# PEER expert layers: all activation tiles computed in the routing stage, and an output stage that streams V alone

## The chip, the cores and the metric

The kernel runs on one core of one Trainium2 chip. The metric is device microseconds of one launch. The engines are called here by the profile's names: PE (TensorE; its weight loads are PEld), DVE (VectorE), ACT (ScalarE), POOL (GpSimd) and SP, which only issues DMAs. DMAs are also issued from the queues of ACT and, for gathers by index, of POOL.

## The reference, cut to what matters

The model has two layers over 512 tokens of width 1024: an mLSTM mixer with a PEER expert layer behind it, then stick-breaking attention with a second PEER layer. The change touches the two PEER layers alone. Of 16384 experts (128 x 128 pairs of sub-keys) each token takes 16 in each of 8 heads:

```python
s = jnp.einsum('thpk,pnk->thpn', q, sub_keys)            # 8 heads, 2 sub-key sets, 128 keys
s_top, i_top = lax.top_k(s, 16)
cand = (s_top[:, :, 0, :, None] + s_top[:, :, 1, None, :]).reshape(128, 8, 256)
g_top, pos = lax.top_k(cand, 16)
expert = jnp.take_along_axis(cand_idx, pos, axis=-1)      # cand_idx = i0 * 128 + i1
g = jax.nn.softmax(g_top, axis=-1)
u = jnp.take(peer_u, expert, axis=0)
act = jax.nn.gelu(jnp.einsum('thkd,td->thk', u, xb), approximate=False)
vv = jnp.take(peer_v, expert, axis=0)
return jnp.einsum('thk,thkd->td', g * act, vv)
```

## The kernel before, in words

All of it is float32. A large product is made of three matmuls in a reduced float type: each operand is split into a high part and a remainder (`whi` and `wlo` of a weight, `hh` and `hl` of an activation, `Wh` and `Wl`), and high x high, high x remainder and remainder x high are summed. ACT makes the high part (L98), POOL or DVE the remainder (L99), as the call says.

A PEER layer, `peer(l)`, treats its tokens in two ways. The first 128 tokens (`NGT = 1` tile) are **gathered**: 128 indirect DMAs on POOL fetch one row of U each per token, DVE takes the dot products with the token (L958, into `uw`), and 128 more fetch rows of V, which DVE adds up with weights (L969, into `yt`). Each fetch is 128 rows of 4 KB into one of four `rows` buffers. The other 384 tokens are computed **densely**: the experts come in 128 tiles `a` of 128. For each tile, 24 matmuls of 384 columns give the scores of its experts (L787, into `pp`) and ACT applies GELU (L790, into `ga` or `sp`): here this is called an act. The routing weights of the dense tokens are spread out to a table `Gd` in DRAM. For each token the one-hot of its second key (`oB`) is multiplied with the one-hot of the first key, scaled by the high and the low half of the weight (`oH`, `oL`): two matmuls of 128 columns (L921, L922, into `gps`); ACT copies four tokens at a time to `stg` (L924), and 32 tokens go to `Gd` in one DMA. At last, per tile, `W = ga * gb` with `gb` read back from `Gd` (L995), and 18 matmuls of 512 columns add W times V to the output (L1016, into `y`), two halves of the width for three token tiles.

The layer runs in three parts:

- The query part: 16 projections (L115), scores (L829), and the top 16 of each by `max`, `max_index` and `match_replace` on DVE (`top16`, L656 to L660).
- The **routing stage**, in which PE and DVE keep the order of the program text. `route` (L662 to L755) is a generator: the program advances it by estimated microseconds. First comes the route of token tile 1. Then 48 steps (16 for each token tile 1 to 3, 8 tokens each): the four one-hot tiles on DVE (`oB`, `oA`, `oH`, `oL`, L910 to L913), 2 us of the next tile's `route`, `run(22)`, which emits 22 of the act matmuls, and the 16 matmuls of these 8 tokens. The next tile's route is that of tile 2, of tile 3, and last that of the gathered tile 0. 56 of the 128 acts (`KPRE`) are made in this stage; the first 10 (layer 0) or 18 (layer 1) stay in SBUF, the others go to DRAM (`spd`).
- The **output stage**, ordered by a scheduler: 128 times 18 matmuls of `y`, with the other 72 acts between them, three tiles ahead, and all 256 gathers spread over it. U is loaded for those 72 acts, V for all tiles, both by `wload` (`wraw`, three buffers, split into `whi` and `wlo`, three buffers).

In the first layer a few steps of the next layers' conditioning (`ada`) run along in the background.

## Time and profile before

| what | value |
|---|---|
| three runs | 3381.13, 3384.81, 3403.76 us; median 3384.81 |
| the profiled execution, first to last instruction | 3385.6 us |
| routing stage of layer 0: first act to first `y` matmul | 484.9 to 862.8 us |
| output stage of layer 0: first to last `y` matmul | 862.8 to 1708.6 us |
| the same of layer 1 | 2172.1 to 2539.3, and 2539.3 to 3375.2 us |
| PE busy over the span | 94% |

The profiled span lies 0.8 us from the median, so a sum in the profile's times can be set against the median directly. "Busy" of PE counts modelled matmul ends, and consecutive matmuls overlap; the distance between starts says how fast they follow each other. The granted clock is 1.00 where TensorE had 2.4 GHz throughout, and lower where part of the stretch was granted 1.2 GHz.

### The profile page before, as it was taken

Reading aid. Unit: us, or ns where it says so; the run is one execution under the profiler, and the core shown is the slowest. Engines: PE = TensorE matmul, PEld = TensorE weight load, DVE = VectorE, ACT = ScalarE, POOL = GpSimd, SP = SyncE. Lnnn points to the kernel's source line nnn. Section 1 sums busy time; section 2 is a strip of 40 time slices with the busy share of each in tenths; the row PEclk is TensorE's granted clock in tenths of the full one; section 3 lists DMA queues with packets and bytes.
Section 4 is the critical chain, followed back from the end, with each engine's and each line's share of the span. In section 5 each row is a group of like instructions: output and inputs, shape, how many; then the busy total and the mean of one; then the engine's idle time right before and its main releaser. Section 6 shows DMA issues by size and latency. Waiting matters only on the chain. (4 is left out here: it accounts for less than half of the span.)

```text
span 3385.6 us, 44234 instructions
## 1 busy us (share of the span) xinstructions
PE 3168.3 (94%) x16160; PEld 2704.2 (80%) x16160; DVE 2655.0 (78%) x4484; ACT 1360.5 (40%) x1898; POOL 1729.5 (51%) x1097
## 2 busy tenths in 40 slices
PE   6899998888999999999989999988889999999999
PEld 5746787888888888888867657978888888888888
DVE  6833699998678888888874484899967888888887
ACT  4254324555333333333342453345543333333333
POOL 3434433343456566566553454433344665666664
PEclk9989998999999999999989899989999999999999
DMA  5621453555889999999955102235568999999997
GB/s 194 212 87 44 158 181 125 184 207 194 293 306 328 330 320 326 340 332 317 324 171 192 44 12 78 94 125 192 203 211 292 315 319 320 327 335 336 328 346 262
DMA packets 308363, 787.62 MB, mean 233 GB/s; under 512 B 25136, under 2 KB 145200, under 8 KB 305072
## 3 DMA queue, kind: packets, MB, share of 16 engines
q1 hardware_dynamic: 218864, 449.48, 39.6%
q0 software_dynamic: 73728, 268.47, 22.0%
q10 hardware_dynamic: 15552, 66.85, 5.1%
q8 instruction: 126, 2.06, 0.3%
q14 instruction: 93, 0.76, 0.1%
HBM read 715.76 MB, written 68.94 MB: 232 GB/s over the span
## 5 line engine op out<-in xcount | busy, mean ns | idle before, releaser
L99 POOL TENSOR_TENSOR wlo<-wraw,whi 128x1024 fp32r<-128x1024 f32 x353 | 894.5, 2535 | 1077.4 <-ACT whi L98 1018.5
L98 ACT CAST whi<-wraw 128x1024 fp32r<-128x1024 f32 x609 | 639.3, 1051 | 899.8 <-PE pp L787 230.6
L787 PE MATMUL pp<-hh,wlo 128*128 128x384 f32 x2048 | 704.7, 344 | 9.8 <-POOL wlo L99 9.6
L787 PE MATMUL pp<-hh,whi 128*128 128x384 f32 x2048 | 703.5, 343 | 10.9 <-ACT whi L98 5.2
L787 PE MATMUL pp<-hl,whi 128*128 128x384 f32 x2048 | 701.9, 343 | 0.0
L1016 PE MATMUL y<-wlo,Wh 128*128 128x512 f32 x1536 | 481.5, 392 | 3.4 <-DVE wlo L99 3.2
L1016 PE MATMUL y<-whi,Wl 128*128 128x512 f32 x1536 | 469.2, 392 | 5.8 <-DVE Wl L99 5.8
L958 DVE SCALAR_TENSOR_TENSOR rows<-rows,htok 128x1024 f32<-128x1024 f32 x256 | 380.4, 1497 | 116.5 <-DMA rows<-in_u_rows,pidx 116.1
L1016 PE MATMUL y<-whi,Wh 128*128 128x512 f32 x1536 | 456.8, 393 | 10.2 <-ACT Wh L98 6.4
L951 POOL DMA_INDIRECT rows<-in_v,pidx x256 | 342.1, 1336 | 212.2 <-DVE yt L969 170.2
L951 POOL DMA_INDIRECT rows<-in_u_rows,pidx x256 | 338.9, 1324 | 153.8 <-DVE rows L958 109.6
L787 PEld LDWEIGHTS pp<-hh,wlo 128*128 128x128 f32 x2048 | 395.5, 193 | 22.9 <-POOL wlo L99 18.1
L787 PEld LDWEIGHTS pp<-hh,whi 128*128 128x128 f32 x2048 | 395.4, 193 | 22.7 <-ACT whi L98 6.1
L969 DVE SCALAR_TENSOR_TENSOR yt<-rows,uw,yt 128x1024 f32<-128x1024 f32 x254 | 367.9, 1448 | 49.9 <-DMA rows<-in_v,pidx 47.8
L787 PEld LDWEIGHTS pp<-hl,whi 128*128 128x128 f32 x2048 | 395.5, 193 | 4.6
L99 DVE TENSOR_TENSOR wlo<-wraw,whi 128x1024 fp32r<-128x1024 f32 x256 | 328.7, 1284 | 63.1 <-ACT whi L98 62.5
L1016 PEld LDWEIGHTS y<-whi,Wh 128*128 128x128 f32 x1536 | 287.0, 189 | 67.9 <-ACT Wh L98 10.3
L1016 PEld LDWEIGHTS y<-whi,Wl 128*128 128x128 f32 x1536 | 288.4, 188 | 65.6 <-DVE Wl L99 8.1
L1016 PEld LDWEIGHTS y<-wlo,Wh 128*128 128x128 f32 x1536 | 288.4, 188 | 62.7 <-DVE wlo L99 5.1
L98 ACT CAST Wh<-W 128x384 fp32r<-128x384 f32 x256 | 130.8, 514 | 477.8 <-DVE W L995 462.6
L115 PE MATMUL pp<-hh,whi 128*128 128x512 f32 x584 | 236.9, 413 | 28.0 <-ACT cbuf L349 9.2
L924 ACT ACTIVATE stg<-gps 128x512 f32<-128x512 f32 x192 | 197.5, 1139 | 140.2 <-PE gps L922 137.9
(282 smaller groups left out, 4508.3 us busy)
## 6 DMA issues: line engine op xcount, KB each, us to landing
wraw<-in_u SPq DMA_DIRECT2D x256, 512.0 KB
wraw<-in_v SPq DMA_DIRECT2D x256, 512.0 KB
g<-stg ACTq DMA_DIRECT2D x24, 2048.0 KB
gb<-g SPq DMA_DIRECT2D x64, 768.0 KB
araw<-in_ada_w SPq DMA_DIRECT2D x80, 512.0 KB
wraw<-in_peer_q SPq DMA_DIRECT2D x32, 512.0 KB
spd<-ga ACTq DMA_DIRECT2D x84, 192.0 KB
ga<-spd SPq DMA_DIRECT2D x84, 192.0 KB
```

The lines of the kernel that those rows point to most:

```text
L98: S.copy(hi, src)
L99: eng.tensor_tensor(lo, src, hi.bitcast(F32), op=OP.subtract)
L115: PE.matmul(ps, a[:, ws], b[k][:, t0:T], start=n == 0, stop=n == 3 * KD - 1)
L787: PE.matmul(ps[:, :ND], p[:, ws], q[k][:, T0:T], start=n == 0, stop=n == 3 * KD - 1)
L924: S.activation(stg[:, :, k:k + 4].rearrange("p a t -> p t a"), gps, AF.Copy, scale=1.0 / GSCALE)
L951: tc.keep_in_program_order(G.indirect_dma_start(out=r, out_offset=None, in_=rows, in_offset=bass.IndirectOffsetOnAxis(ap=pidx[i][:, n:n + ...
L958: V.scalar_tensor_tensor(r, r, 1.0, htok[i], op0=OP.mult, op1=OP.mult, accum_out=uw[i][:, n:n + 1])
L969: V.scalar_tensor_tensor(yt[i], r, uw[i][:, n:n + 1], yt[i], op0=OP.mult, op1=OP.add)
L1016: PE.matmul(y[t][d], wa[:, ts], vb[:, d * 512:(d + 1) * 512], start=n == 0 and i == 0, stop=n == NA - 1 and i == 2)
```

## The change

Six things change in `peer(l)`, and nothing outside it but comments.

1. All 128 acts are made in the routing stage. `fetch` loads U and casts the high part two acts ahead; the 24 matmuls of an act and its GELU are as before. Results go to DRAM in groups of four tiles; layer 0 keeps none in SBUF, layer 1 two groups (8 acts).
2. The remainder of U is made on DVE (`remainder`), at a place in DVE's order that the program fixes: half an act into each act, for the act two later. Before, POOL made it.
3. The gathered tile 0 is routed first, so its U rows are gathered in the routing stage: 7 while tile 1 is routed, the others at two or three a step. Each step's rows are used (the dot products) in the next step. The V rows stay in the output stage.
4. Only `oA` and `oB` stay on DVE. `oH` becomes 8 instructions of 128 columns a step on POOL, `oL` 8 on ACT. The placing matmuls (`place`) come one step late, in the middle of the next step's 54 act matmuls.
5. `Gd` is laid out by groups of four tiles. A write of 32 tokens now goes out as 32 pieces of 512 bytes from each partition, where it was one of 16 KB; a read of one group is 6 KB from each partition in one piece, where it was twelve of 512 bytes.
6. The output stage has no acts. It reads `gb` and `ga` (768 KB each) once per four tiles, one group ahead, and takes the tiles in order.

```diff
-KPRE = 56
-UROUTE = (250, 230)
-UCHUNK = 22
+NGRP = NA // 4
+GROW = NSUB * 128 + 32
+UCHUNK = 54
 RCHUNK = 2.0
-KSBS = (10, 18)
-DEPTH = 3
+KEEP = (0, 2)
+ROWS = 4
...
-            ap = st.enter_context(tc.tile_pool(name="pact", bufs=2))
+            ap = st.enter_context(tc.tile_pool(name="pact", bufs=3))
...
-                hi, lo = wload(U[a], G)
...
-            def early_acts():
-                for a in range(KPRE):
-                    if a < KSB:
-                        yield from act_steps(a, spill[a])
-                    else:
-                        ga = ap.tile([128, ND], F32, name="ga")
-                        yield from act_steps(a, ga)
-                        nc.scalar.dma_start(spd[a - KSB], ga)
...
+            plan = [("u", n) for n in range(128)] + [("v", n) for n in range(128)]
+            flight = []
+            yt = []
+            def issue():
+                kind, n = plan.pop(0)
+                r = kp.tile([128, D], F32, name="rows", bufs=ROWS)
+                tc.keep_in_program_order(G.indirect_dma_start(
+                    out=r, out_offset=None, in_=Ur if kind == "u" else Vr,
+                    in_offset=bass.IndirectOffsetOnAxis(ap=pidx[:, n:n + 1], axis=0)))
+                flight.append((kind, n, r))
+            def use():
+                kind, n, r = flight.pop(0)
+                if kind == "u":
+                    V.scalar_tensor_tensor(r, r, 1.0, htok, op0=OP.mult, op1=OP.mult, accum_out=uw[:, n:n + 1])
+                    if n == 127:
+                        S.activation(uw, uw, AF.Gelu)
+                        V.tensor_tensor(uw, uw, pg, op=OP.mult)
+                elif n == 0:
+                    V.tensor_scalar(yt[0], r, uw[:, 0:1], None, op0=OP.mult)
+                else:
+                    V.scalar_tensor_tensor(yt[0], r, uw[:, n:n + 1], yt[0], op0=OP.mult, op1=OP.add)
...
-                acts = early_acts()
...
+                def fetch():
+                    if nxt[0] == NA:
+                        return
+                    raw = wp.tile([128, 1024], F32, name="wraw")
+                    nc.sync.dma_start(raw, U[nxt[0]])
+                    hi = wp.tile([128, 1024], F32R, name="whi", bufs=HLB)
+                    S.copy(hi, raw)
+                    parts.append([raw, hi, None])
+                def remainder():
+                    for p in parts:
+                        if p[2] is None:
+                            p[2] = wp.tile([128, 1024], F32R, name="wlo", bufs=HLB)
+                            V.tensor_tensor(p[2], p[0], p[1].bitcast(F32), op=OP.subtract)
+                def all_acts():
+                    for a in range(NA):
+                        _, hi, lo = parts.pop(0)
+                        fetch()
+                        ps = pp()
+                        n = 0
+                        for k in range(KD):
+                            ws = slice(k * 128, (k + 1) * 128)
+                            for p, q in ((hi, h[0]), (hi, h[1]), (lo, h[0])):
+                                PE.matmul(ps[:, :ND], p[:, ws], q[k][:, T0:T], start=n == 0, stop=n == 3 * KD - 1)
+                                n += 1
+                                if n == 3 * KD // 2:
+                                    remainder()
+                                if n == 3 * KD:
+                                    if a // 4 < keep:
+                                        S.activation(held[a // 4][:, a % 4], ps[:, :ND], AF.Gelu)
+                                    else:
+                                        ga = ap.tile([128, ND], F32, name="ga")
+                                        S.activation(ga, ps[:, :ND], AF.Gelu)
+                                        nc.scalar.dma_start(spd[a // 4][:, (a % 4) * ND:(a % 4 + 1) * ND], ga)
+                                yield
...
+                fetch()
+                fetch()
+                remainder()
+                run(12)
...
+                gen = gathered()
+                while advance(gen, 3.0):
+                    run(24)
                 gen = routed(NGT)
-                advance(gen, 24)
-                run(UROUTE[l])
-                advance(gen, 1e9)
-                for i in range(NGT):
-                    for q in range(2):
-                        ps = pp()
-                        for k in range(4):
-                            c = slice(i * 128, (i + 1) * 128)
-                            for n in range(2):
-                                PE.matmul(ps[:, k * 128:(k + 1) * 128], h[n][4 * q + k][:, c], identr, start=n == 0, stop=n == 1)
-                        S.copy(htok[i][:, q * 512:(q + 1) * 512], ps)
+                while advance(gen, 3.0):
+                    run(24)
+                    while flight:
+                        use()
+                    issue()
...
+                        return bc(s[:, o:o + CHUNK][:, :, None, :], CHUNK, 64, 2)
+                    oB = gp.tile([128, CHUNK, 128], F16, name="oB", bufs=3)
+                    oA = gp.tile([128, CHUNK, 128], F16, name="oA", bufs=2)
+                    oH = gp.tile([128, CHUNK, 128], F16, name="oH", bufs=2)
+                    oL = gp.tile([128, CHUNK, 128], F16, name="oL", bufs=2)
+                    V.tensor_tensor(pairs(oA), i4, dup(aT), op=OP.is_equal)
+                    V.tensor_tensor(pairs(oB), i4, dup(bT), op=OP.is_equal)
+                    for n in range(CHUNK):
+                        G.tensor_scalar(oH[:, n], oA[:, n], gh[:, o + n:o + n + 1], 1.0, op0=OP.mult, op1=OP.mult)
+                        S.activation(oL[:, n], oA[:, n], AF.Copy, scale=gl[:, o + n:o + n + 1])
+                    return oB, oH, oL
+                def place(s, c, stg, oB, oH, oL):
+                    for j in range(CHUNK // 4):
+                        gps = pq.tile([128, 4, 128], F32, name="gps", bufs=2)
+                        for i in range(4):
+                            n = 4 * j + i
+                            PE.matmul(gps[:, i], oB[:, n], oH[:, n], start=True, stop=False)
+                            PE.matmul(gps[:, i], oB[:, n], oL[:, n], start=False, stop=True)
+                        k = c * CHUNK + 4 * j
+                        S.activation(stg[:, :, k:k + 4].rearrange("p a t -> p t a"), gps, AF.Copy, scale=1.0 / GSCALE)
+                    if c == 32 // CHUNK - 1:
+                        nc.scalar.dma_start(Gd[:, :, s * 128:(s + 1) * 128].rearrange("g p c -> p g c"),
+                                            stg.rearrange("p (g a) t -> p g (a t)", a=4))
...
+                late, done, steps = None, 0, (4 - NGT) * 128 // CHUNK
+                left = len(plan) - 128
                 for t in range(NGT, 4):
-                    gen = routed(t + 1) if t < 3 else gathered(0)
-                    aT, bT, gh, gl = heads[t]
+                    gen = routed(t + 1) if t < 3 else iter(())
                     for sub in range(4):
-                            V.tensor_tensor(pairs(oB), i4, dup(bT), op=OP.is_equal)
-                            V.tensor_tensor(pairs(oA), i4, dup(aT), op=OP.is_equal)
-                            V.tensor_tensor(pairs(oH), pairs(oA), dup(gh), op=OP.mult)
-                            V.tensor_tensor(pairs(oL), pairs(oA), dup(gl), op=OP.mult)
+                            ones_of = expand(t, sub * 32 + c * CHUNK)
                             advance(gen, RCHUNK)
                             tick(1 if c != 1 else 0)
-                            run(UCHUNK)
-                            for j in range(CHUNK // 4):
...
-                        nc.scalar.dma_start(Gd[(t - NGT) * 4 + sub, :, 0:128 * 32], stg.rearrange("p a t -> p (a t)"))
+                            while flight:
+                                use()
+                            done += 1
+                            while len(plan) > 128 and len(plan) - 128 > left * (1 - done / (steps - 2)) and len(flight) < ROWS:
+                                issue()
+                            run(UCHUNK // 2)
+                            if late:
+                                place(*late)
+                            run(UCHUNK - UCHUNK // 2)
+                            late = ((t - NGT) * 4 + sub, c, stg, *ones_of)
                     advance(gen, 1e9)
-                run(24 * KPRE)
+                run(24 * NA)
...
+                def weights(g):
+                    gb = vp.tile([128, NSUB, 4, 32], F32, name="gb")
+                    nc.sync.dma_start(gb.rearrange("p s a t -> p (s a t)"), Gd[g, :, 0:NSUB * 128])
+                    if g < keep:
+                        ga = held[g]
                     else:
-                        V.scalar_tensor_tensor(yt[i], r, uw[i][:, n:n + 1], yt[i], op0=OP.mult, op1=OP.add)
...
-                def gload(g):
-                    gbs[g] = vp.tile([128, NSUB, 128], F32, name="gb")
-                    nc.sync.dma_start(gbs[g], Gd[:, :, g * 128:(g + 1) * 128].rearrange("s p c -> p s c"))
...
+                    V.tensor_tensor(W.rearrange("p a (s t) -> p a s t", t=32), ga.rearrange("p a (s t) -> p a s t", t=32),
+                                    gb.rearrange("p s a t -> p a s t"), op=OP.mult)
+                    Wh = vp.tile([128, 4, ND], F32R, name="Wh")
+                    Wl = vp.tile([128, 4, ND], F32R, name="Wl")
                     split(Wh, Wl, W, V)
                     return Wh, Wl
...
+                ready = [weights(0)]
+                for a in range(NA):
                     vh, vl = wload(Vw[a], V)
-                    Wh, Wl = ready.pop(0)
-                    if n + DEPTH < NA:
-                        ready.append(weights(flat[n + DEPTH]))
-                        step += flat[n + DEPTH] >= KPRE
...
```

On DVE, in the routing stage of layer 0, a step with the end of a tile's `route` (`eq`, `ab`) and the start of the next one stood so before:

```order
L910 TENSOR_TENSOR oB<-iota,bT 128x1024
L911 TENSOR_TENSOR oA<-iota,aT 128x1024
L912 TENSOR_TENSOR oH<-oA,gh 128x1024
L913 TENSOR_TENSOR oL<-oA,gl 128x1024
L738 TENSOR_TENSOR eq<-eq,t_4443 128x2048
L740 TENSOR_TENSOR eq<-eq 128x128x8
L742 TENSOR_TENSOR eq<-eq 128x128x4
L745 TENSOR_REDUCE ab_4512<-eq 128x128
L910 TENSOR_TENSOR oB<-iota,bT 128x1024
L911 TENSOR_TENSOR oA<-iota,aT 128x1024
```

And the same place now (`rows,uw` is the dot product with a gathered row):

```order
L960 TENSOR_TENSOR oA<-iota,aT 128x1024
L961 TENSOR_TENSOR oB<-iota,bT 128x1024
L738 TENSOR_TENSOR eq<-eq,t_5084 128x2048
L740 TENSOR_TENSOR eq<-eq 128x128x8
L742 TENSOR_TENSOR eq<-eq 128x128x4
L745 TENSOR_REDUCE ab_5222<-eq 128x128
L798 SCALAR_TENSOR_TENSOR rows,uw<-rows,htok 128x1024 x3
L861 TENSOR_TENSOR wlo<-wraw,whi 128x1024 x3
L960 TENSOR_TENSOR oA<-iota,aT 128x1024
L961 TENSOR_TENSOR oB<-iota,bT 128x1024
```

Two one-hot tiles have left DVE's step, and two or three dot products and two or three remainders of U have come in behind the stretch of `route`.

On SP, at the passage from the routing to the output stage of layer 0, the loads stood so before (`in_v` is V, `in_u` U, `gb` the read of `Gd`):

```order
L103 DMA wraw<-in_u 128x1024 x40
L103 DMA wraw<-in_v 128x1024
L103 DMA wraw<-in_u 128x1024
L981 DMA gb<-g_2264 128x12x128 x2
L103 DMA wraw<-in_v 128x1024 x5
L981 DMA gb<-g_2264 128x12x128
L103 DMA wraw<-in_u 128x1024
```

And now (`ga` is the read of the stored acts):

```order
L851 DMA wraw<-in_u 128x1024 x105
L1020 DMA gb<-g_2264 128x1536
L1025 DMA ga_10799<-spd_0_2275 128x1536
L103 DMA wraw<-in_v 128x1024
L1020 DMA gb<-g_2264 128x1536
L1025 DMA ga_10845<-spd_1_2276 128x1536
L103 DMA wraw<-in_v 128x1024
```

The first load of V now stands behind the first read of `Gd`, which needs the last write to it, and the second behind the second group's reads; U is over by then.

## Rows read from the trace of the kernel before

**Rows 1.** Stretches: busy us (count) per engine, granted clock, DMA share, GB/s.
```profile
485.00:863.00 378.00, 329.88 (x2252) 315.85 (x2251) 347.62 (x750) 194.56 (x232) 148.89 (x58) 0.92 0.51 179
863.00:1709.00 846.00, 825.72 (x3962) 720.97 (x3961) 709.38 (x775) 295.46 (x400) 518.68 (x327) 1.00 0.92 320
...
2539.00:3376.00 837.00, 822.87 (x3969) 722.88 (x3967) 692.16 (x769) 292.35 (x396) 509.88 (x324) 1.00 0.92 319
2950.00:3350.00 400.00, 395.13 (x1912) 347.40 (x1911) 348.64 (x319) 142.75 (x192) 253.16 (x160) 1.00 0.96 335
```

**Rows 2.** Chain of waits in layer 1's routing stage, shares by line.
```profile
by line: DVE oH L912 12.1%; PE pp L787 11.9%; DVE oB L910 10.7%; DVE oA L911 10.2%; DVE oL L913 10.0%; DVE eq L733 3.3%; DVE px L657 2.9%; DVE cd L658 2.8%; DVE px L660 2.8%; DVE eq L738 2.6%; DVE eq L740 2.6%; DVE gt L659 2.3%; issue 1.8%;
```

**Rows 3.** Order of time in layer 1's routing stage: start us, us, instruction.
```profile
2300.07 0.33 PE L787 MATMUL pp<-hh,whi 128*128 128x384 f32 x1
...
2300.27 0.68 DVE L911 TENSOR_TENSOR oA<-iota,aT 128x1024 f16<-128x1024 f16 x1
...
2302.74 2.39 POOL L99 TENSOR_TENSOR wlo<-wraw,whi 128x1024 fp32r<-128x1024 f32 x1 [2.95 <-ACT whi L98]
2302.80 2.88 DVE L911 TENSOR_TENSOR oA<-iota,aT 128x1024 f16<-128x1024 f16 x1
2302.84 0.33 PE L787 MATMUL pp<-hl,whi 128*128 128x384 f32 x1
...
2303.20 0.23 PE L921 MATMUL gps<-oH,oB 128*128 128x128 f16 x1
...
2304.05 0.22 PE L922 MATMUL gps<-oL,oB 128*128 128x128 f16 x1
```

**Rows 4.** Order of time in layer 1's output stage, PE alone.
```profile
2699.69 0.62 PE L1016 MATMUL y<-whi,Wl 128*128 128x512 f32 x2
...
2702.89 1.29 PE L1016 MATMUL y<-whi,Wh 128*128 128x512 f32 x5
```

**Rows 5.** DVE by line: ns min/median/max, first and last start us.
```profile
L99 DVE TENSOR_TENSOR wlo<-wraw,whi x256: 1208/1218/4076, 855.6 to 3369.4; 128x1024 fp32r<-128x1024 f32 x128
...
L958 DVE SCALAR_TENSOR_TENSOR rows<-rows,htok x256: 1206/1219/3968, 869.3 to 2965.2; 128x1024 f32<-128x1024 f32 x128
L958 DVE DVE_READ_ACCUMULATOR rows<-rows,htok x256: 71/80/85, 870.5 to 2966.3; 128x1 f32 x128
...
L969 DVE SCALAR_TENSOR_TENSOR yt<-rows,uw,yt x254: 1269/1280/3952, 1299.3 to 3368.2; 128x1024 f32<-128x1024 f32 x127
...
L667 DVE TENSOR_TENSOR cd<-tv x32: 209/214/2187, 501.4 to 2416.7; 128x64 f32<-128x64 f32 x32
```

**Rows 6.** Stretch of tile 1's route in layer 0, columns as before.
```profile
501.40:542.90 41.50, 32.52 (x173) 31.42 (x171) 38.79 (x110) 12.85 (x18) 19.27 (x8) 0.92 0.31 102
```

**Rows 7.** POOL and ACT by line and form: busy us, mean ns, idle before.
```profile
L951 POOL DMA_INDIRECT rows<-in_u_rows,pidx x256 | 338.9, 1324 | 153.8 <-DVE rows L958 109.6 <-issue 35.3 <-DVE wlo L99 2.2
L598 POOL TENSOR_SCALAR_AFFINE_SELECT m<-m 128x128 f32<-128x128 f32 x64 | 33.5, 524 | 5.6 <-ACT m L597 4.5
...
masks.py:199 POOL TENSOR_SCALAR_AFFINE_SELECT ident<-ident 128x128 f32<-128x128 f32 x1 | 0.3, 282 | 0.0
...
L98 ACT CAST whi<-wraw 128x1024 fp32r<-128x1024 f32 x609 | 639.3, 1051 | 899.8 <-PE pp L787 230.6 <-issue 172.7 <-DMA wraw<-in_v 138.0
L924 ACT ACTIVATE stg<-gps 128x512 f32<-128x512 f32 x192 | 197.5, 1139 | 140.2 <-PE gps L922 137.9 <-ACT ga L790 2.1
...
L790 ACT ACTIVATE ga<-pp 128x384 f32<-128x384 f32 x228 | 110.8, 486 | 90.7 <-PE pp L787 89.5 <-ACT stg L924 0.9
...
L420 ACT ACTIVATE Dm<-rb,cols 128x128 f32<-128x128 f32 x48 | 14.6, 356 | 0.0
```

**Rows 8.** The page, part 6: DMA issues, KB each.
```profile
wraw<-in_u SPq DMA_DIRECT2D x256, 512.0 KB
...
g<-stg ACTq DMA_DIRECT2D x24, 2048.0 KB
...
spd<-ga ACTq DMA_DIRECT2D x84, 192.0 KB
```

More of the change, by code (lines that the diff above doesn't have):

```diff
@@ new lines, in peer @@
+                fetch()
+                remainder()
+                run(12)
+                for q in range(2):
+                    ps = pp()
+                    for k in range(4):
+                        for n in range(2):
+                            PE.matmul(ps[:, k * 128:(k + 1) * 128], h[n][4 * q + k][:, 0:128], identr, start=n == 0, stop=n == 1)
+                    S.copy(htok[:, q * 512:(q + 1) * 512], ps)
+                gen = gathered()
+                while advance(gen, 3.0):
+                    run(24)
@@ L917, in peer @@
-                            for j in range(CHUNK // 4):
-                                gps = pq.tile([128, 4, 128], F32, name="gps", bufs=2)
-                                for i in range(4):
-                                    n = 4 * j + i
-                                    PE.matmul(gps[:, i], oB[:, n], oH[:, n], start=True, stop=False)
-                                    PE.matmul(gps[:, i], oB[:, n], oL[:, n], start=False, stop=True)
-                                k = c * CHUNK + 4 * j
-                                S.activation(stg[:, :, k:k + 4].rearrange("p a t -> p t a"), gps, AF.Copy,
-                                             scale=1.0 / GSCALE)
@@ L947, in peer @@
-                yt = [vp.tile([128, D], F32, name=f"yt{i}", bufs=1) for i in range(NGT)]
-                def gather(rows, i, n):
-                    r = vp.tile([128, D], F32, name="rows", bufs=4)
-                    tc.keep_in_program_order(G.indirect_dma_start(
-                        out=r, out_offset=None, in_=rows,
-                        in_offset=bass.IndirectOffsetOnAxis(ap=pidx[i][:, n:n + 1], axis=0)))
-                    return r
-                def gather_u(i, n):
-                    r = gather(Ur, i, n)
-                    V.scalar_tensor_tensor(r, r, 1.0, htok[i], op0=OP.mult, op1=OP.mult, accum_out=uw[i][:, n:n + 1])
@@ L983, in weights @@
[L983 to L998 removed]
+                yt.append(vp.tile([128, D], F32, name="yt", bufs=1))
```

134 lines of the change are left out of this document (48 added, 86 removed).

## The prediction

> **What bounds the kernel now.** I cut the span into its stages and read each by itself, since the 94% of PE is a mean over stages with different limits. First comes the view of stretches [rows 1]. In the output stages (863 to 1709 and 2539 to 3376 us) PE is busy for nearly the whole stretch at a granted clock of 1.00, its full 2.4 GHz, and the DMA engines are busy for 92% at 319 to 320 GB/s; in the best 400 us it is 96% at 335 GB/s. In the routing stage DVE is busy for 348 of 378 us, PE less, the clock is 0.92 (some of it was granted 1.2 GHz), and the DMA engines idle for half of the time. The chain of waits in that stage [rows 2] says who sets its pace: the four one-hot lines of DVE hold 43% of it and acts of PE 12%. So there are a stage bound by DVE that leaves PE and DMA idle, and one in which PE and DMA are both close to full.
>
> How full is read from the distance between starts. Sixteen act matmuls lie between 2300.07 and 2302.84, so one takes 0.173 us; fifteen placing matmuls between 2303.20 and 2304.05, 0.057 each [rows 3]; fourteen `y` matmuls between 2699.69 and 2702.89, 0.229 each [rows 4]. A layer needs 3072 x 0.173 = 531, 768 x 0.057 = 44 and 2304 x 0.229 = 528 us of PE, 1103 together. From the first act to the last `y` matmul layer 0 takes 1708.6 - 484.9 = 1224 us and layer 1 1203. So 121 and 100 us a layer, 221 in all, is everything that a better order on PE could win. Nearly all of it lies in the routing stage: in the output stage 1728 x 0.173 + 528 = 827 of 846 us are needed.
>
> DVE's routing time is partly not its own. A one-hot tile takes 0.68 us, but 2.88 when it starts 0.06 us behind a POOL remainder of 2.39, and ends after it [rows 3]. The Trainium skill, page "SBUF — State Buffer", section "SBUF: two separate sides", has the rule for it: DVE instructions with two SBUF inputs and GpSimd instructions share a port pair that whichever starts first holds to its end. The trace agrees with that, and the rule is weighed below, since the change puts other work on POOL.
>
> **The change part by part.** *Start of the routing stage.* DVE is done with the top-16 scans at 501.4 us in layer 0 and then begins `route` [rows 5]; PE's first act is at 484.9. Now three remainders stand among those scans, 3 x 1.22 = 3.7 us [rows 5], and two routes come before the steps. A route took 41.5 us with 38.8 of DVE busy beside 19.3 of POOL remainders [rows 6]: without those it is between 38.8 - 19.3 = 19.5 and 38.8, and I take 30, about the middle, since scans ran on beside POOL. With 12 more remainders (14.6) and 6 dot products of 1.22 + 0.08 us [rows 5] DVE needs 82 us from 505 on, to 587. PE waits for these remainders: it can have run about 15 acts by then, 62 of 102 us. So the start costs PE some 40 us, which is the largest single loss of the new order. Layer 1 has the same beginning; as far behind its first act as in layer 0 (587 - 485 = 102 us behind 2172), that is 2274.
>
> *A step.* PE has 54 x 0.173 + 16 x 0.057 = 10.3 us. DVE has two one-hot tiles (1.4), on average 1.25 of route (two routes in 48 steps), 2.5 dot products (3.3) and 2.25 remainders (2.7): 8.7 us. ACT has 2.25 x (1.05 + 0.49), two copies of 1.14 and eight `oL`, whose nearest row is 128 columns with a scale per partition at 0.36 [rows 7]: 8.6. POOL has 2.5 gathers of 1.32 and eight `oH`; no row shows that form, the nearest are 128-column selects between 0.28 and 0.52 [rows 7]: 5.6 to 7.5. None of these is the longest. DMA has 2.25 loads of U and 2.5 gathers of 0.524 MB, 2.25 stored acts of 0.197 and a quarter of a 2.1 MB write [rows 8], 3.5 MB in all: at 328 GB/s 10.6 us. So a step is set by DMA and PE together, just over 10 us, where before it was set by DVE.
>
> *Output stage.* PE has 18 x 0.229 = 4.1 us a tile. DMA has V and a gathered row block (1.05 of 128 / 122), and a quarter of 768 + 768 KB: 1.47 MB, at 328 GB/s 4.5 us. DVE has a remainder 1.22, a weighted row 1.28 [rows 5] and a quarter of two products of 1536 columns; it is not near. The stage becomes bound by DMA.
>
> *Sum.* From the end of the start on, layer 0 still moves 58 MB of U (111 tiles), 64 of gathered U, 22 of stored acts, 25 to the table; then 67 of V, 67 of gathered V, 25 from the table and 25 of acts: 354 MB; layer 1, which keeps 8 acts, 351. PE still has 2712 x 0.173 + 44 + 528 = 1041 us. The rate is the term that I choose. The rows give 319 (mean of an output stage) and 335 (best 400 us); both were taken with PE full, so neither is shown to be a limit, and no row shows that rate with one part in five written. I take 328, near the middle: 1080 and 1070 us, so DMA and not PE sets the pace, by 3 to 4%. To this come bubbles. In the first step PE waits for one-hot tiles, route and dot products before the next remainder, some 6 us. At the passage 156 act matmuls (27 us) cover two copies, the last table write, the first two reads and the product, about 18 us by the same rows; but DMA has little to do there, and the first loads of V stand behind those reads on SP, so I allow 10. Layer 0 ends at 587 + 1080 + 16 = 1683 instead of 1708.6, 26 us sooner; layer 1 at 2274 + 1070 + 16 = 3360 instead of 3375.2, 15 sooner. Query part, mixers and the tail stay. 3385.6 - 41 = 3345 us, and the span is 0.8 us from the median of the runs, so this is the forecast. At 335 GB/s with 10 us of bubbles it is 3288, at 319 with 20 it is 3413.
>
> **The rivals.** *PE alone sets the pace.* If DMA takes whatever it is asked for (353 GB/s in the output stage), each layer takes the start, 1041 us and 16 of bubbles: 1644 and 3331, 3277 us. For it speaks that the loads are now larger (6 KB pieces instead of twelve of 512 bytes); against it, that no stretch reached that rate [rows 1].
>
> *The table write holds ACT's queue.* This one ends on the other side. Stored acts stand behind the 2.1 MB table writes on the same queue, now 32 pieces of 512 bytes from each partition instead of one of 16 KB, and with the other queues full, where they were half idle [rows 1]. GELU has three buffers, some 14 us at 4.7 us an act; when the store of an act is later than that, GELU waits, ACT's casts of U behind it too, and PE soon after. With the queue's third of 328 GB/s the write takes 19 us, 5 too many; twelve writes a layer make 60 us, alone it takes 6 and costs nothing. From 2 us a write on (24 a layer) the change loses. At 40 us a layer it is 3425.
>
> *POOL's `oH` holds up DVE.* If each of the 8 instructions of a step keeps DVE waiting for its whole length (0.40, the middle of its bounds), DVE has 8.7 + 3.2 = 11.9 us a step, 1.3 over DMA's 10.6, 62 us a layer: 3469. It decides from 0.24 us of waiting for each of them. The port rule quoted above is this rival's ground. Against it: the scans of `route` ran beside POOL's remainders [rows 6], each lasts a sixth of a remainder, and POOL may be the one that waits.
>
> *It comes out even.* The sustained rate is 320 GB/s, that of today's output stages: 354 and 351 MB take 1106 and 1097 us, and with the start and the bubbles nothing is left of the gain: 3398.
>
> **How the numbers follow.** Forecast (3300 to 3380): 0.44. PE alone (3300 or less): 0.19. Even (3380 to 3410): 0.12. Queue (3400 to 3460): 0.17. POOL's hold (about 3469): 0.08. The range 3265 to 3445 leaves out the far end of the first rival and of the last two. A change of this kernel is told from none at about 1%, 34 us. Faster than 3351 are the PE rival and two thirds of the forecast, 0.48; slower than 3419 are POOL's hold and most of the queue's, 0.22; the remaining 0.30 lies between.
>
> **What would show it.** In the new profile: the first `y` matmul of layer 0 near 1130 us and the last near 1683; a DMA share over 0.9 in steps and output stage alike; PE's waits in the output stage ended by loads of V; PE starved until about 587 us and little after it; the clock at 1.00 in the steps. PE's waits for `oH` or for remainders in the steps would speak for POOL's hold; GELU waiting for stores, for the queue. I am wrong if writing 512-byte pieces costs more than its bytes, or if DVE's order makes the remainders late behind a gather that has not landed: three of its instructions wait for gathers in each step, and the remainders of U, for which PE waits, are queued behind them.

## The result, and the profile after

The changed kernel takes 3586.23 us (median of 4 runs, 3584.45 to 3589.89) against 3387.18 us before: a ratio of 1.0589, with a 95% interval of 1.0555 to 1.0623. It is 6% slower; 3345 was forecast, and the range ended at 3445. The profiled execution has a span of 3582.7 us. By stages:

| layer 0, us | before | forecast | changed |
|---|---|---|---|
| first act of PE | 484.9 | 485 | 477.5 |
| first one-hot tile of the steps, on DVE | 542.9 | 587 | 581.9 |
| first `y` matmul | 862.8 | 1130 | 1212.8 |
| last `y` matmul | 1708.6 | 1683 | 1802.5 |

In layer 1 the same marks are 2271.3, 2366.8, 2992.9 and 3572.2. First act to last `y` takes 1325 and 1301 us, where it took 1224 and 1203. The start of the routing stage, from the first act to the first one-hot tile of the steps, is about as forecast (104 and 96 us for 102). In layer 0 the steps with the last acts take 631 us for 543, and the output stage 590 for 553.

The view of stretches, with the columns of [rows 1] (busy us of PE, PEld, DVE, ACT and POOL, then granted clock, DMA share and GB/s): the two stages of layer 0, then parts of its output stage, and last two short stretches of a step in layer 1.

```profile
478.00:1213.00 735.00, 625.04 (x3881) 607.11 (x3880) 504.21 (x1049) 407.96 (x752) 409.00 (x520) 0.92 0.77 258
1213.00:1802.00 589.00, 545.09 (x2327) 440.10 (x2327) 407.99 (x317) 181.52 (x167) 189.35 (x122) 0.98 0.82 309
1220.00:1640.00 420.00, 379.72 (x1596) 303.32 (x1595) 324.35 (x253) 127.19 (x116) 182.49 (x119) 0.97 0.92 352
1650.00:1802.00 152.00, 149.85 (x661) 123.52 (x660) 69.60 (x53) 53.54 (x50) 4.46 (x2) 1.00 0.53 183
...
2424.00:2432.00 8.00, 0.00 (x0) 0.00 (x0) 3.69 (x7) 3.35 (x10) 4.21 (x4) 0.79 1.12 356
2432.40:2435.40 3.00, 2.93 (x9) 2.94 (x10) 0.89 (x1) 2.33 (x4) 0.00 (x0) 0.50 0.84 278
```

The routing stage does not run at the DMA engines' pace (share 0.77), nor at DVE's (504 of 735 us). The output stage falls in two: until about 1640 the DMA engines carry 352 GB/s and PE is busy for 90%; from 1650 on PE is full and the DMA engines are half idle. And there are stretches of some 8 us in which PE does nothing at all, followed by 3 us at a granted clock of 0.50, its 1.2 GHz.

The first kind of loss is seen from the distance of PE's placing blocks. Of 92 steps (worked out from the starts of these blocks) 67 last 10.6 us on average, most of them 10.3, which is PE's own sum in the forecast; 25 last over 14, 18.2 on average. 20 of these 25 come every fourth step, behind a table write. The order of time of ACT and its queue (ACTq) around one of them, in layer 1 (start us, us, instruction, idle time before it):

```profile
2413.76 2.10 ACT L976 ACTIVATE stg<-gps 128x512 f32<-128x512 f32 x2
2415.89 0.38 ACTq L978 DMA_DIRECT2D g<-stg  x1
...
2417.65 0.49 ACT L881 ACTIVATE ga<-pp 128x384 f32<-128x384 f32 x1
2418.04 1.04 ACT L853 CAST whi<-wraw 128x1024 fp32r<-128x1024 f32 x1
2418.17 10.44 ACTq L882 DMA_DIRECT2D spd<-ga  x1
2428.65 2.44 ACT L964 ACTIVATE oL<-oA,gl 128x128 f16<-128x128 f16 x8 [9.58 <-DVE rows L798]
```

The table write itself takes 0.38 us to issue. The store of the next act, behind it on the same queue, takes 10.44, and ACT starts nothing until it is out. The idle time is put down to `rows`, DVE's dot product, but that had ended at 2427.7 and writes nothing that `oL` reads; what really ended it is the row above. All stores by line (ns min/median/max) show the same, then the page's part 6 (KB each, median us to landing):

```profile
L882 ACTq DMA_DIRECT2D spd<-ga x248: 326/326/11685, 488.3 to 2999.9; - x124
```

```profile
g<-stg ACTq DMA_DIRECT2D x24, 2048.0 KB, 17.9
...
spd<-ga ACTq DMA_DIRECT2D x248, 192.0 KB, 4.7
```

Most stores are issued in 0.33 us; 24 of them, one behind each write, take 5.0 to 11.7, 221 us in all. This is called the hold below, and a piece is one contiguous run of a transfer. In the kernel before no issue on ACT's queue took over 0.4 us. But SP's queue showed a hold already then: behind a read of `gb`, which was 12 x 128 = 1536 pieces of 512 bytes, loads took up to 4.9 us to issue, 17 of them over 2 us. In the kernel before (start us, us, instruction):

```profile
852.18 1.57 SPq L981 DMA_DIRECT2D gb<-g  x2
853.92 4.19 SPq L103 DMA_DIRECT2D wraw<-in_v  x2
```

In the changed kernel PE feels the hold through GELU and the casts of U. PE's waits (total us, times, longest), in the steps and in the first part of the output stage of layer 0, and PE's order of time behind the hold:

```profile
PE pp L872 <- ACT ga L881: 55.3, 11, 7.9
PE pp L872 <- DVE wlo L861: 11.7, 6, 4.4
...
PE y L1048 <- ACT whi L98: 22.4, 11, 3.3
PE y L1048 <- DVE wlo L99: 17.9, 18, 2.7
```

```profile
2432.47 0.69 PE L872 MATMUL pp<-hh,whi 128*128 128x384 f32 x1 [8.87 <-ACT ga L881]
2432.95 0.52 PE L872 MATMUL pp<-hl,whi 128*128 128x384 f32 x1
2433.27 0.52 PE L872 MATMUL pp<-hh,wlo 128*128 128x384 f32 x1
...
2435.68 0.34 PE L872 MATMUL pp<-hl,whi 128*128 128x384 f32 x1
2435.85 0.34 PE L872 MATMUL pp<-hh,wlo 128*128 128x384 f32 x1
```

PE waits 8.87 us for GELU's buffer `pp`, then starts its matmuls 0.32 us apart instead of the 0.173 of [rows 3], until the clock is back. In the chain of waits around this write, ACT's queue stands in the place that DVE's one-hot lines had in [rows 2]:

```profile
by line: PE pp L872 29.5%; ACTq L882 23.8%; DMA wraw<-in_u 15.8%; issue 6.2%; ACT oL L964 5.3%; ACT stg L976 5.0%; ACT whi L853 4.8%; ACT ga L881 3.4%; ACT L881 3.2%; PE gps L973 1.2%; PE gps L974 1.1%; ACTq L978 0.9%; ACT L680 0.8%; ACT eg
```

What DVE now does beside POOL is not held up: the remainder by line (ns min/median/max) has a longest of 1.38 us, where [rows 5] had 4.08, and `oA` 0.77, where [rows 3] has 2.88. POOL's `oH`, the last row, is quick in the median, but its longest is 2.43 us.

```profile
L861 DVE TENSOR_TENSOR wlo<-wraw,whi x256: 1203/1221/1384, 474.1 to 2983.7; 128x1024 fp32r<-128x1024 f32 x128
...
L960 DVE TENSOR_TENSOR oA<-iota,aT x96: 676/684/772, 581.9 to 2951.6; 128x1024 f16<-128x1024 f16 x96
...
L963 POOL TENSOR_SCALAR oH<-oA,gh x768: 364/370/2427, 582.7 to 2956.3; 128x128 f16<-128x128 f16 x192
```

### The profile page after: what moved, and what is told of

It reads as the page before. It is cut to its first block, busy times and chain, and to the rows that moved or that the text cites. A ratio compares the mean times of both kernels' runs of the same rounds, so it can differ in the third digit from the quotient of the medians.

```text
span 3582.7 us, 45302 instructions
## 1 busy us (share of the span) xinstructions
PE 3204.5 (89%) x16160; PEld 2725.7 (76%) x16160; DVE 2388.9 (67%) x4170; ACT 1562.0 (44%) x2474; POOL 1593.8 (44%) x1609
## 5 line engine op out<-in xcount | busy, mean ns | idle before, releaser
L872 PE MATMUL pp<-hh,whi 128*128 128x384 f32 x2048 | 725.9, 354 | 128.8 <-ACT ga L881 128.5
L963 POOL TENSOR_SCALAR oH<-oA,gh 128x128 f16<-128x128 f16 x768 | 469.4, 627 | 375.9 <-DVE oA L960 353.5
L790 POOL DMA_INDIRECT rows<-in_v,pidx x256 | 388.3, 1517 | 532.1 <-DVE yt L805 471.7
L872 PEld LDWEIGHTS pp<-hh,whi 128*128 128x128 f32 x2048 | 406.8, 199 | 137.6 <-ACT ga L881 137.4
L1048 PE MATMUL y<-whi,Wl 128*128 128x512 f32 x1536 | 479.9, 394 | 0.0
L861 DVE TENSOR_TENSOR wlo<-wraw,whi 128x1024 fp32r<-128x1024 f32 x256 | 309.1, 1225 | 235.2 <-ACT whi L853 234.8
L1048 PE MATMUL y<-whi,Wh 128*128 128x512 f32 x1536 | 420.9, 395 | 48.1 <-ACT whi L98 48.1
L99 POOL TENSOR_TENSOR wlo<-wraw,whi 128x1024 fp32r<-128x1024 f32 x97 | 251.5, 2598 | 476.2 <-ACT whi L98 471.7
L798 DVE SCALAR_TENSOR_TENSOR rows<-rows,htok 128x1024 f32<-128x1024 f32 x256 | 313.5, 1243 | 186.6 <-DMA rows<-in_u_rows,pidx 186.3
L99 DVE TENSOR_TENSOR wlo<-wraw,whi 128x1024 fp32r<-128x1024 f32 x256 | 311.0, 1220 | 149.8 <-ACT whi L98 149.3
L805 DVE SCALAR_TENSOR_TENSOR yt<-rows,uw,yt 128x1024 f32<-128x1024 f32 x254 | 325.9, 1283 | 37.1 <-DMA rows<-in_v,pidx 35.0
## 6 DMA issues: line engine op xcount, KB each, us to landing
g<-stg ACTq DMA_DIRECT2D x24, 2048.0 KB, 17.9
```

The lines of the kernel that those rows point to most:

```text
L99: eng.tensor_tensor(lo, src, hi.bitcast(F32), op=OP.subtract)
L790: tc.keep_in_program_order(G.indirect_dma_start(out=r, out_offset=None, in_=Ur if kind == "u" else Vr, in_offset=bass.IndirectOffsetOnAxis ...
L798: V.scalar_tensor_tensor(r, r, 1.0, htok, op0=OP.mult, op1=OP.mult, accum_out=uw[:, n:n + 1])
L805: V.scalar_tensor_tensor(yt[0], r, uw[:, n:n + 1], yt[0], op0=OP.mult, op1=OP.add)
L861: V.tensor_tensor(p[2], p[0], p[1].bitcast(F32), op=OP.subtract)
L872: PE.matmul(ps[:, :ND], p[:, ws], q[k][:, T0:T], start=n == 0, stop=n == 3 * KD - 1)
```

## The experiments

Theory A: the store behind a write of 4096 pieces is held at its issue, and with it ACT. Theory T (called B in e1's expectation), close to the forecast's view: there is too much traffic for the DMA engines. Theories C (small pieces are dear in themselves), G (gathers awaited by DVE) and E (gathers crowded in the output stage) came in as rows called for them. Ratios are to the kernel before, run beside each experiment, with 95% intervals.

| run | us | ratio |
|---|---|---|
| e1_old_layout | 3529 | 1.041 (1.036 to 1.046) |
| e2_stores_on_sp | 3483 | 1.026 (1.021 to 1.030) |
| e3_write_on_sp | 3524 | 1.039 (1.034 to 1.043) |
| e4_split_write | 3468 | 1.022 (1.017 to 1.027) |
| e5_no_gather_wait | 3444 | 1.015 (1.008 to 1.023) |
| e6_split_old | 3487 | 1.027 (1.021 to 1.034) |
| e7_rolling | 3448 | 1.016 (1.010 to 1.021) |
| e8_rolling_even | 3352 | 0.989 (0.984 to 0.994) |
| e9_even_alone | 3483 | 1.028 (1.025 to 1.031) |
| e10_whole_write | 3466 | 1.021 (1.017 to 1.025) |
| e11_quarter_writes | 3357 | 0.989 (0.986 to 0.991) |
| e12_half_writes | 3387 | 1.000 (0.998 to 1.002) |
| e13_pinned_only | 3502 | 1.033 (1.029 to 1.037) |

**Is it the queue?** Four ways around the hold, each alone.

```diff
 e1: the table as before
-nc.scalar.dma_start(Gd[:, :, s * 128:(s + 1) * 128].rearrange("g p c -> p g c"), ...)
+nc.scalar.dma_start(Gd[s, :, 0:128 * 32], stg.rearrange("p a t -> p (a t)"))
 e2: the stores on SP's queue
-nc.scalar.dma_start(spd[a // 4][...], ga)
+nc.sync.dma_start(spd[a // 4][...], ga)
 e3: the table write on SP's queue
-nc.scalar.dma_start(Gd[:, :, s * 128:...
+nc.sync.dma_start(Gd[:, :, s * 128:...
 e4: one write of 32 groups becomes four of 8, one a step
+gs = slice(q * NGRP // 4, (q + 1) * NGRP // 4)
+nc.scalar.dma_start(Gd[gs, :, s * 128:(s + 1) * 128]..., stg...[:, gs])
```

> Edit: the table in its layout of before (a write is one piece of 16 KB from each partition again, a read of one group 12 pieces of 512 bytes), all else as in the changed kernel. Theory A, the hold at the issue: after each table write of 4096 pieces the next store on ACT's queue takes 9 to 11 us to issue and keeps ACT's casts, oL and copies behind it; 24 such steps last about 18.7 us where the others last 10.3, some 200 us. It expects no hold here and 3586 - 200 = 3386 us (3365 to 3410), steps of 10.3 us throughout. Theory B, the traffic: the steps are long because 25 MB more are written and 12 MB of stored acts more per layer, whatever the pieces; it expects 3560 to 3590.

> Edit: the stores of the acts are issued on SP's queue, the table writes stay on ACT's queue in 512-byte pieces. Theory A (hold at the issue of the next DMA on the same queue): nothing stands behind a table write on ACT's queue for 41 us, it lands in 18, so ACT is not held: 3386 us (3370 to 3430; the stores may now hold up SP's loads a little). Theory C, the small pieces themselves are dear (they take DMA engine time and slow all other transfers): still 18 us for each fourth step, 3550 to 3590.

> Edit: the table writes are issued on SP's queue, the stores stay on ACT's. Theory A: the hold moves to SP, to the next load of U, which then starts 8 to 10 us late; loads run two acts ahead (2 x 4.6 us), so most but not all of it is covered, and PE loses 2 to 5 us a write: 3386 + 24 x 3.5 = 3470 us (3430 to 3510), with the long times on SP's issues and none on ACT's. Theory C: 3550 to 3590.

> Edit: each table write is cut into four of 1024 pieces (8 groups each), issued one a step; same pieces, same bytes, same queue. Theory A with a queue that holds a limited number of pieces: a write of 1024 has drained before the next (10 us later), holds of under 2.5 us that fall into ACT's idle time: 3390 us (3375 to 3430). If instead any write of small pieces keeps the next store waiting until all of it has landed, whatever its size, each of 96 pieces holds 4 to 5 us and about half of it shows: 3450 to 3550. Theory C: 3550 to 3590.

All four are faster than the change, so theory T in its first form (3560 or more) falls, and with e2 and e4, which still write 512-byte pieces, so does C. In e1, e2 and e4 the long issues of stores are gone, as A says (e4's time lies in the band of its second case, but no store is held there; only four of its writes, issued one behind the other at the end of a layer, took 2.4 to 3.7 us). In e3 the hold has moved to SP, whose loads of U behind a write are held:

```profile
636.87 0.39 SPq L978 DMA_DIRECT2D g<-stg  x1
637.36 13.86 SPq L851 DMA_DIRECT2D wraw<-in_u  x3
```

But all four miss the bands that A gave them (3365 to 3430, and 3430 to 3510 for e3). In e1 the steps behind a write still take about 16 us, though no issue on ACT's queue lasts over 1.2. PE's and DVE's waits there (600 to 1130 us), and two lines of the chain behind a write in layer 1:

```profile
PE pp L872 <- DVE wlo L861: 47.7, 19, 6.7
...
DVE rows L798 <- DMA rows<-in_u_rows,pidx: 120.1, 46, 7.8
```

```profile
2384.61 13.55 DMA rows<-in_u_rows,pidx
...
2399.41 2.27 DVE wlo L861 x2
```

A gather that shares the DMA engines with the write takes 13.55 us to land; DVE waits for it with the dot product, and the remainders that PE needs stand behind that. A second wait was hidden behind the first. e1 also brings back the reads of `gb` in 1536 pieces, and with them a hold on SP at the start of each output stage: ten issues of over 2 us, 57 us in all, where the change has none there. The first of them:

```profile
1167.63 0.65 SPq L1019 DMA_DIRECT2D gb<-g  x1
1168.33 9.31 SPq L1024 DMA_DIRECT2D ga<-spd  x1
```

**Is it the gathers?** e5 takes that wait away, on the layout of e1. e6 cuts the write of e1 in four. e7 uses a fetched row only when all four buffers are full, on top of e6.

```diff
 e5: nobody reads the fetched row (the gathered tile's scores are left out)
-V.scalar_tensor_tensor(r, r, 1.0, htok, ...)
+V.scalar_tensor_tensor(junk[0], htok, 1.0, htok, ...)
 e6: four writes of 4 KB pieces, one a step
+nc.scalar.dma_start(Gd[s, :, q * 1024:(q + 1) * 1024], stg[:, q * 32:(q + 1) * 32]...)
 e7: the use rolls
-while flight:
-    use()
 ...
+    if len(flight) == ROWS:
+        use()
     issue()
```

> Edit: the table in its old layout (as in the first experiment), and the dot products of the gathered tile read the token's own row twice instead of the fetched row, so that all gathers still run but nobody waits for them; the gathered tile's scores are left out by this. Theory G: in the first experiment, with the hold on ACT gone, PE waits for remainders of U (48 of 530 us in layer 0), which are queued on DVE behind dot products that wait for gathers (120 us); it expects steps of 10.3 to 10.6 us, the last act of layer 0 near 1120 us instead of 1183, and 3529 - 2 x 55 = 3420 us (3395 to 3445). Theory T (the traffic in the steps is too much for the DMA engines, whoever waits): U comes late instead, steps of 11.5 us or more, 3490 to 3530.

> Edit: old layout of the table, and each write cut into four of 4 KB from each partition, issued one a step. Theory A says that only the number of pieces in one issue matters for ACT, and theory G that a shorter burst makes the gathers less late: as the fourth experiment with its 512-byte pieces, 3468 us (3445 to 3490), no issue on ACT's queue over 1 us. Theory C (small pieces are dear in themselves) expects this one clearly faster than the fourth, by 30 us or more: 3400 to 3440.

> Edit: as the sixth, and the gathers of U roll: a fetched row is used only when all four buffers are full, just before the next fetch, so that a fetch has about 1.5 steps (16 us) to land instead of under 1. Theory G: PE's waits for remainders in the steps go, steps of 10.3 to 10.7 us on average where the fourth and sixth have about 11.3, 20 to 30 us a layer: 3468 - 50 = 3418 us (3395 to 3445). Theory T: no gain, 3455 to 3490.

e5 came to 3444, at the end of what G expects and far from T: the wait for gathers was worth 86 us of e1. Its steps took 11.1 us on average, not 10.3 to 10.6. PE's waits of 600 to 1130 us show what is next:

```profile
PE gps L975 <- POOL oH L965: 10.5, 14, 1.5
PE pp L873 <- ACT ga L882: 4.1, 4, 2.3
PE pp L873 <- DVE wlo L862: 4.0, 6, 1.0
```

e6 is no faster than e4 (3487 against 3468), so writing smaller pieces costs the kernel no time once the bursts are short: steps last 11.4 us on average in both. The 19 us between them lie in the output stages (594 and 587 us in e6, 576 and 582 in e4), where e6 reads `gb` in 1536 pieces again and SP's issues last up to 9.7 us; no run was made on this. The pieces do cost DMA engine time: ACT's queue moves the same 99 MB in 7.6% of the engines' span in e6 and in 8.9% in e4. e7 gains 39 us on e6; steps are 11.0 on average, a little over what G expected, and the total missed its band by 3 us.

**The output stage.** e8 pins the weighted rows of V to their place in DVE's order, on top of e7. e9 is the same edit on the changed kernel, e13 the pin without the longer distance between fetch and use.

```diff
 e8, e9 and e13
-V.scalar_tensor_tensor(yt[0], r, uw[:, n:n + 1], yt[0], ...)
+tc.keep_in_program_order(V.scalar_tensor_tensor(yt[0], r, uw[:, n:n + 1], yt[0], ...))
 e8 and e9
-    issue()
-    use()
+    if len(flight) == ROWS - 1:
+        use()
+    issue()
```

> Edit: as the seventh, and in the output stage the weighted rows of V keep their place in DVE's order, 1.05 to a tile, with four fetches in flight, where they ran ahead at 1.37 a tile and were over at tile 93. Theory E (the output stage is slow because the gathers are crowded into its first 430 us, where the DMA engines carry 345 GB/s and PE waits for V, while they are half idle in the last 150): 184 MB fit into 535 to 560 us, the output stage shrinks from 580 to about 552, 3418 - 56 = 3362 us (3335 to 3390), and the kernel is faster than before. Theory T2 (the stage is bound by DMA over its whole length): 3405 to 3440.

> Edit: the changed kernel with one thing of the eighth experiment alone: in the output stage the weighted rows of V keep their place in DVE's order (1.05 to a tile, four fetches in flight); layout, writes and routing stage stay as in the change. Theory E (crowded gathers cost 45 us of each output stage): 3586 - 90 = 3496 us (3475 to 3520), output stages of 545 to 560 us. Theory T2 (that gain needs the calmer routing stage of the eighth): 3560 to 3590.

> Edit: the changed kernel, with the weighted rows of V kept at their place in DVE's order and nothing else (each row is still used by the instruction right behind its fetch in the program, where the ninth experiment has up to three other fetches between). Theory E (the crowding of the gathers into the first 430 us of each output stage is what costs): as the ninth, 3483 us (3465 to 3505). Theory W (DVE's waits for rows fetched too late hold up the remainders of V, as they did in the routing stage, and the longer distance between fetch and use was the cure): 3540 to 3590.

In the changed kernel nearly all of the 128 rows were used by tile 93, 1.37 a tile; pinned, they last to the end. DVE's weighted rows in the output stage of layer 0 (ns min/median/max, first and last start us; the last `y` starts at 1802 and 1746), the change first, then e9:

```profile
L805 DVE SCALAR_TENSOR_TENSOR yt<-rows,uw,yt x124: 1271/1280/1324, 1214.7 to 1648.6; 128x1024 f32<-128x1024 f32 x124
```

```profile
L805 DVE SCALAR_TENSOR_TENSOR yt<-rows,uw,yt x127: 1274/1280/1324, 1221.6 to 1738.9; 128x1024 f32<-128x1024 f32 x127
```

The output stages shrink from 590 and 579 us to 539 and 537 in e9, and to 546 and 543 in e13: the crowding is the cause of some 84 of the 103 us. The other 19 may go with the longer distance, but the two intervals overlap. Theory W falls. (e13's 3502 lies within theory E's band, and e9's 3483 within its own.) Here is e8, a steps stretch and two of the output stage, and PE's waits from 1150 to 1650 us:

```profile
600.00:1100.00 500.00, 482.91 (x3215) 469.33 (x3213) 375.96 (x628) 352.51 (x672) 414.67 (x487) 0.99 0.91 321
1150.00:1650.00 500.00, 486.42 (x2110) 396.12 (x2109) 382.13 (x300) 165.72 (x147) 195.65 (x121) 0.99 0.94 342
1300.00:1400.00 100.00, 99.43 (x437) 81.32 (x436) 77.22 (x61) 33.21 (x30) 39.20 (x26) 1.00 0.98 357
```

```profile
PE y L1057 <- ACT whi L98: 7.9, 6, 2.1
PE y L1057 <- DVE wlo L99: 5.7, 6, 1.5
```

PE is busy for 97% of the steps at 321 GB/s, and for 97 to 99% of these stretches of the output stage beside 342 to 357 GB/s. T2 falls. e8 beats both kernels: 1.1% faster than before (0.6 to 1.6).

**The price of the hold, with nothing else in the way.** e10, e11 and e12 are e8 with the change's own layout and the write whole, in quarters and in halves (e4's edit with 1, 4 and 2 for the number of parts).

> Edit: the eighth experiment with the change's own table write (4096 pieces of 512 bytes, undivided). Theory A: the holds of 9 to 10 us come back on each of 24 writes and show as some 8 us of PE each, 3352 + 190 = 3540 us (3500 to 3570), since nothing else in the steps can take them up. Theory G alone (what costs is the wait for gathers behind the burst, which rolling takes away): 3360 to 3400.

> Edit: the eighth experiment with the change's layout (512-byte pieces written, 6 KB pieces read), each write cut into four of 1024 pieces. Theory A: no hold, and no price of the small pieces themselves: as the eighth, 3352 us (3335 to 3370). Theory C (small pieces cost DMA time): 3390 or more.

> Edit: as the eleventh, but each write cut into two of 2048 pieces. In the profile of the changed kernel a write of 4096 pieces lands after 18 us and the store behind it is let go about 12 us after its issue, so some 1200 to 1500 pieces still stood in the queue. If the queue holds that many, a write of 2048 holds the next store for 2 to 4 us, most of it in ACT's idle time: 3352 + 20 = 3372 us (3350 to 3410). If any write over the limit waits for its whole landing: holds of 7 to 9 us, 48 of them, 3450 or more.

The quarters are as fast as e8, so the change's layout is not at fault, only that 4096 pieces go out in one issue. The whole write costs 3466 - 3357 = 109 us, 4.5 a write and not 8: A's price was too high by nearly half, and G alone (3400 at most) falls too. Steps say why: e10's average is 12.3 us, e11's is 11.0, with 2 MB to be written and rows to be awaited in both. A whole write is also a longer burst for the gathers, and no run parts that from the hold; PE's waits do (2200 to 3000 us, e10 first, then e11):

```profile
PE pp L872 <- ACT ga L881: 54.6, 14, 7.4
PE pp L872 <- DVE wlo L861: 15.1, 9, 3.6
```

```profile
PE pp L872 <- DVE wlo L861: 17.9, 14, 3.6
...
PE pp L872 <- ACT ga L881: 12.6, 11, 2.4
```

The wait for ACT is four times as long, and the wait for remainders, behind which the gathers stand, no longer. The waits are only a part of the price, as the stretch of the steps shows (first placing matmul to first `y` of layer 0, e10 and e11):

```profile
596.00:1209.80 613.80, 543.95 (x3474) 530.08 (x3473) 395.72 (x651) 370.79 (x695) 413.01 (x493) 0.94 0.84 285
```

```profile
601.30:1151.30 550.00, 524.42 (x3476) 509.96 (x3475) 396.16 (x651) 371.61 (x695) 419.07 (x493) 0.99 0.94 320
```

Of 64 us, 44 are idle time of PE, and for nearly the same number of matmuls it is also busy for 20 us more, at a mean granted clock of 0.94 where e11 has 0.99. Halves cost 30 us. One of e12's writes and the store behind it, in ACT's order:

```profile
2480.90 0.38 ACTq L984 DMA_DIRECT2D g<-stg  x1
...
2484.26 3.69 ACTq L882 DMA_DIRECT2D spd<-ga  x1
```

28 stores are held for over 2 us there, 4.2 on average: what the run was built on, that a limited number of pieces can stand in a queue, fits; the number itself was not measured.

## Why the prediction was wrong

Two steps of it failed: the sum gave the table write's hold on ACT's queue no time, and it took the gathers of V to be spread evenly over the output stage. The 241 us between 3345 and 3586 are found in the runs: 109 for the hold (e10 to e11), 103 for the crowded output stage (the change to e9), 17 for the rolling use (e9 to e10), and 12 by which e11 still misses the forecast. The prices hold in this order only: rolling was worth 39 us on e6.

- **The start.** Right: the steps begin at 581.9 us (587 forecast) in layer 0, and in layer 1, 96 us behind its first act (102). PE had made 13.5 acts by then, where 15 were counted on.
- **A step.** PE's 10.3 us is exact: most steps last just that. "So a step is set by DMA and PE together" was not borne out: the DMA share was 0.83 in the steps of the change and 0.84 in those of e1, while PE waited; in e8 it is 0.91, with PE at 97%. (By the prediction's own terms 28% of a step's bytes are written, not "one part in five".)
- **The queue: the first step that failed.** In the forecast's sum the steps lose 6 us to bubbles and nothing to the queue. The rival "The table write holds ACT's queue" was what happened. Its sum gave 19 us for a write (17.9 measured, but on the two landings that the trace holds) and 60 us a layer; the runs give 109 / 2 = 55. It was given 40 and a chance of 0.17, on the ground that GELU's three buffers cover most of it. That point was wrong: in the change GELU waited for such a buffer once, for 2.8 us. The issue of the store itself is held, and with it casts, `oL` and copies; and PE, idle for 8.87 us behind the hold shown above, then ran at 1.2 GHz for 3 us. The loads held up behind reads of 1536 pieces on SP's queue could have been seen in the trace before.
- **The output stage: the second step that failed.** The forecast put "a gathered row block (1.05 of 128 / 122)" into every tile, from the program text. On DVE the scheduler had placed 1.37 a tile, which the order of DVE's instructions would have told. Priced by e9: 103 us. It was no case among the rivals.
- **The rate.** "I take 328" chose a limit that is none: the DMA engines carried 352 GB/s over 420 us in the change, and 357 over 100 us in e8 with PE busy for 99%. So "The stage becomes bound by DMA" is wrong where gathers are spread evenly: e8's output stage takes 546 us, against 528 of PE's and the 553 between the forecast's marks, at a mean of 331 GB/s. The argument against the rival "PE alone" (no stretch had reached that rate) fell with it.
- **Bubbles.** 6 us for the steps was too little. The prediction's last sentence named the mechanism (remainders queued behind a gather that has not landed) but gave it no price; by e5 it is 86 us once the hold is gone, while in the changed kernel most of it is hidden behind the hold (with the hold still there, e9 to e10, rolling gains 17).
- **POOL's hold on DVE.** It did not occur, but the reverse did, which the prediction allowed for ("POOL may be the one that waits"). Remainders that ran beside an `oH` took 1.25 us on average, the others 1.22. Of the 768 `oH`, 188 took over 0.6 us, up to 2.43, and every one of these ran beside a DVE instruction with two large inputs (a dot product, `oB`, a remainder); of the other 580 only 10 did. With the rows of before [rows 3], where DVE waited, this agrees with the port rule that the prediction quotes. `oH` had a median of 0.37 us, within the forecast's bounds, and a mean of 0.63, above them. PE's waits for it are 10.5 us of 530 in e5.
- **It does what it says?** With the two orders mended (e8, e11) the time is 3352 and 3357, within 12 us of the forecast, partly by errors that cancel: in layer 0 of e8 the start ends at 587.5 (587), the steps and the last acts take 555 us (543 in the forecast, and PE with its waits sets them and not DMA), the output stage 546 (553). Of the 221 us of idle PE some 190 are left, nearly half of them in the starts (in layer 0, 104 us for 13.5 acts, 56 us of PE); no run worked on that.

## What to carry to other kernels

Count the pieces of a DMA, not only its bytes, and look at what is queued behind it on the engine that issues it: cut a write of thousands of pieces into parts that drain between issues, or give it a queue on which nothing urgent follows. When a row shows an engine idle, look at its own queue's issues before believing the releaser that is named. Read the pace of a background stream from the order of instructions on its engine, not from the loop that was meant to spread it; and when one wait is removed, ask at once what was hidden behind it: here that kept four ways around the hold (3468 to 3529 us) from reaching the time that was expected of them.

## What the hardware showed that was not expected

A DMA issue on ACT's queue lasted up to 11.7 us in the change, and ACT's own instructions behind it waited, though most issues of stores take 0.33 us. It depends on the pieces, not the bytes: 2 MB in pieces of 16 KB (e1) brought no store of over 2 us, four writes of 1024 pieces (e11) two of 2.6 us on average, writes of 2048 pieces 28 of 4.2 us (e12), and of 4096 pieces 24 to 26 of 8.1 to 9.2 (the change and e10). The same happens on SP's queue, behind writes of 4096 pieces (e3) and behind reads of 1536 (the kernel before and e1). The Trainium skill, page "Perfetto Trace Analysis", section "DMA Instruction — HWDGE (DVE, Sync)", says that a DMA instruction occupies its sequencer until its descriptors have been generated, and that there may be more of them than fit in a buffer. The rows agree that an issue can last for microseconds, but not on where: the write of 4096 pieces was out in 0.38 us, and the wait fell on the small store behind it.

An `oH` on POOL of 0.37 us lasted up to 2.43 when it met DVE's instructions with two inputs, while DVE's own kept their pace.

The DMA engines carried 352 GB/s over 420 us with PE busy for 90% (the change) and 357 over 100 us with PE at 99% (e8), where the best 400 us of the trace before had 335.
